# Two two-layer blocks on one core: when the next layer's weights are split, in which order the first rows arrive, and how one value product is formed

## The chip, the cores and the metric

The kernel runs on one core of a Trainium2 chip. The metric is the device time of one execution in microseconds (us). The engines are named as in the profile: PE is TensorE (matrix products), PEld its weight load, DVE is VectorE, ACT is ScalarE, POOL is GpSimd, SP is the engine whose queue issues every DMA of this kernel. A time in the text without a unit is in us from the start of the span.

## The reference

An activation `x` of 512 tokens by 2048 features passes through four layers, two of one block type and then two of another. Each layer is

```
h    = rms_norm(x, g_pre)                 # second block: times (1 + scale), plus shift
proj = h @ w_in                           # 2048 -> 5952 or 5648 columns
o    = several attentions and gates on proj
y    = o @ w_out                          # 2048 -> 2048
x    = x + rms_norm(y, g_post)            # second block: times gate
```

In the second block one of the mixers is a gated linear attention with four heads. Written as one causal product over all 512 tokens, a head's output of 128 tokens is the sum, over the earlier chunks of 128 tokens, of a 128 x 128 score block times the value block of that chunk: 1, 2, 3 and 4 products for the four chunks, 10 for a head. All of it is float32 and has to come out as float32.

## The kernel before

**The products.** A float32 operand is split into a high part that is rounded to the matmul's type (`ACT` copies it) and a low part, the rest (`DVE` subtracts). A product of two split operands is three matmuls: high by high, high by low, low by high (`mm3`, L667). The split of an activation or weight of 128 x 512 costs one ACT and one DVE instruction (`split`, L654). Weights stream from HBM in slots of up to 512 KB into three staging buffers (`st`), are split into `big` tiles or, for a few slots of the first group of a layer, into small tiles `ws`; `Stream.pump` (L563) splits every slot that its window admits and issues the DMAs of the next ones. A staging buffer takes its next DMA only when both parts of its split are done, and SP's queue is in order, so what stands behind that DMA waits too.

**The order of the work.** The program is a single list for each engine, written while the kernel is built. A planner (`Model`, `Side`) keeps an estimated clock for each engine. Large projections are written straight out; between their matmuls `tick` runs steps of side jobs (generators) whose due time has passed. Urgent jobs are run first, about 1 us of planned time after they are due. Only the order comes from the planner; on the chip each engine runs its list in order and waits for semaphores.

**Between layers.** The last quarter of `w_out` (`o3`) and the first group of the next layer (`a_k`, 256 columns, 16 tiles of 128 features, four slots of weights) are computed by blocks of 128 tokens, block 0 to 3 (`by_tokens`, L719). For a block, `o3` takes 48 matmuls of 512 columns (eight slots of weights) and `a_k` 48 of 256. When a block of `o3` is out, an urgent `chain` (L904) is added: the norm after the layer (`y` from `y`, `m`, `x`), four sums of squares on ACT for the next layer's norm, its scaling (`x` from `y`, `m`, `row`), and for each 512 features four transposes on PE, the high part on ACT (`Xh`) and the low part on DVE (`Xl`). Block b of `a_k` needs chain b. In block 3 of `o3`, after each of its eight slots, `pump` splits the weights of `a_k` (L746 to L748).

**The opening.** `first_x` (L845) issues the DMAs of the four blocks of `x` and of the gain rows and the first weights, in the order x0, gain rows, x1, two weight slots, x2, a third slot; then writes the whole norm and transposition of block 0, the sums of squares of block 1, the split of the first weight slot, and the DMA of x3. `pre` (L816) is that norm: four sums of squares on ACT, scaling on DVE (`h`), transposes, split. The jobs of blocks 1 to 3 are independent of each other and run from the ticks of `a_k`.

**The value product of the linear attention.** `out` (L1948) splits the values `V` of a head into a high and a low tile and forms the 10 products with `mm3`, so 30 matmuls of 128 columns, into one PSUM bank; one ACT copy of 128 x 512 takes it out (`og`). There are eight such heads in the kernel, four in each layer of the second block.

Of the kernel before, what the change touches and what calls it, by code (L numbers as in the profile page):

```python
# [9 lines left out]
F32R = mybir.dt.float32r  # L10
I32 = mybir.dt.int32
AF = mybir.ActivationFunctionType
ALU = mybir.AluOpType
# [146 lines left out]
NPAD = 1  # L160
MODT = 1000.0
SHARE = 30.0
BUSY = 0.75
TICK = 3.41333
LOG = None
# [199 lines left out]
class Side:  # L365
# [46 lines left out]
    def step(self, jobs, force):  # L412

        m = self.model
        now = m.clock["PE"]
        nxt = None
        for j in jobs:
            t = j.at()
            spare = (SPARE1 if j.stage else SPARE0) if not force else 0 if j.stage else 4
            if t is None or not self.space(j, 0 if j.urgent else spare):  # L420
                continue
            if t + (SEM if force else SLACK) <= now and (force or j.urgent or self.fits(CAP) and m.free("at", 4, now + 0.1)):
                self.run_one(j)
                return None
            nxt = t if nxt is None else min(t, nxt)
        return -1.0 if nxt is None else nxt

    def start(self, rate):

# [66 lines left out]
class Stream:  # L496
# [86 lines left out]
    def load(self, n):  # L583
        while self.dp < n:
            self.dma(self.items[self.dp])
            self.dp += 1
# [12 lines left out]
class Kern:  # L599
# [119 lines left out]
    def by_tokens(self, parts, need=None, sides=False):  # L719

        st = self.stream
        its = [[] for p in parts]
        self.side.keep = 0
        ahead = NW + 1 if sides else NW
        st.hold = True
        for b in range(4):
            if need and b == 3:
                st.hold = False
            if need:
                self.side.finish([need[b]])  # L730
                self.model.clock["PE"] = max(self.model.clock["PE"], need[b].ready)
            c = slice(b * 128, b * 128 + 128)
            for p, ((spec, evac), mine) in enumerate(zip(parts, its)):
                n, slots = spec
                last = slots[-1][0] + slots[-1][1] - 1
                ps = self.pj()
                for i, (k0, kc, off) in enumerate(slots):
                    if b == 0:
                        mine.append(st.take(sides and 0 < i < 4))
                        st.pump(ahead)  # L740
                    for k2 in range(kc):
                        k = k0 + k2
                        self.mm3(ps[:, :n], [t[:, c] for t in self.Xk(k)], mine[i]["hl"][k2], k == 0, k == last)
                        if k < last:
                            self.side.tick()
                    if b == 3:  # L746
                        st.used(mine[i])
                        st.pump(ahead)  # L748
                evac(b, ps)
                self.side.tick()  # L750
        self.side.keep = SPAREM
# [61 lines left out]
        return f  # L813


    def pre(self, s, xn, tmp, nxt):  # L816

        nc = self.nc
        ss = self.m(4)
        for j in range(4):  # L820
            nc.scalar.activation(self.junk, xn[j], AF.Square, accum_out=ss[:, j:j + 1])
        tot = self.m(1)
        nc.vector.tensor_reduce(tot, ss, axis=AX.X, op=ALU.add)
        r = self.rstd(tot, 1, 1.0 / D)
        yield
        sh = nxt.get("shift")
        for j in range(4):
            nc.vector.scalar_tensor_tensor(tmp[j], xn[j], r, nxt["rows"][j], op0=ALU.mult, op1=ALU.mult)
        for j in range(4):
            yield tmp[j]  # L830
            ps = self.at()
            for i in range(4):
                self.tr(ps[:, i * 128:i * 128 + 128], tmp[j][:, i * 128:i * 128 + 128])
            cs = slice(s * 128, s * 128 + 128)
            xh, xl = self.Xh[:, j * 4:j * 4 + 4, cs], self.Xl[:, j * 4:j * 4 + 4, cs]
            if sh is None:
                self.split(xh, xl, ps.rearrange("p (k t) -> p k t", k=4))
            else:
                cols = [(i, ps[:, i * 128:i * 128 + 128], sh[:, j * 4 + i:j * 4 + i + 1]) for i in range(4)]
                for i, p, c in cols:  # L840
                    nc.scalar.activation(xh[:, i], p, AF.Identity, bias=c)
                for i, p, c in cols:
                    nc.vector.scalar_tensor_tensor(xl[:, i], p, c, xh[:, i].bitcast(F32), op0=ALU.add, op1=ALU.subtract)

    def first_x(self, nxt):  # L845
        nc, I = self.nc, self.I
        xs = [[] for s in range(4)]

        def load(s):
            for j in range(4):  # L850
                t = self.s(name="x")
                nc.sync.dma_start(t, I["x"][s * 128:s * 128 + 128, j * 512:j * 512 + 512])
                xs[s].append(t)

        load(0)
        nxt = nxt()
        load(1)
        self.stream.load(2)
        load(2)
        self.stream.load(3)  # L860
        tmp = [[self.s(name="h") for j in range(4)] for s in range(4)]
        jobs = [self.side.add(self.pre(s, xs[s], tmp[s], nxt), urgent=True) for s in range(4)]

        while not jobs[0].done:
            self.side.run_one(jobs[0])
        self.side.run_one(jobs[1])
        self.stream.pump(1)
        load(3)
        return jobs

    def out_proj(self, PL, l, gains, resid, sink, nxt):

# [677 lines left out]
    def block2(self, l, nxt, chains):  # L1550
        nc, I, side = self.nc, self.I, self.side
# [5 lines left out]
        cs = lambda i: slice(i * 128, i * 128 + 128)  # L1557
# [26 lines left out]
        half = [slice(0, 64), slice(64, 128)]  # L1584
# [258 lines left out]
        cv = [None] * 4  # L1843
# [42 lines left out]
        def gla(dch, after):  # L1886
# [61 lines left out]
            def out(hh):  # L1948
                h = 2 * dch + hh
# [11 lines left out]
                yield  # L1961
                ad = self.hl(name="ad")
                self.split(ad[0], ad[1], A[hh])
                V = self.hl((128, 4, 128), name="V")
                self.split(V[0], V[1], cv[h])
                yield
                blk = lambda t_, i: (t_[0][:, cs(i)], t_[1][:, cs(i)])
                terms = [
                    [(0, blk(ad, 0))],
                    [(1, blk(ad, 1)), (0, blk(fa, 0))],  # L1970
                    [(2, blk(ad, 2)), (0, blk(fa, 1)), (1, blk(fb, 0))],
                    [(3, blk(ad, 3)), (0, blk(fa, 2)), (1, blk(fb, 1)), (2, blk(fa, 3))],
                ]
                ps = self.at()
                for c in range(4):
                    for j, (s, a) in enumerate(terms[c]):
                        self.mm3(ps[:, cs(c)], a, (V[0][:, s], V[1][:, s]), j == 0, j == len(terms[c]) - 1)
                t = self.s(name="og")
                nc.scalar.activation(t, ps, AF.Copy)
                yield  # L1980
                ss = self.m(4)
                junk = self.junk
# [211 lines left out]
```

## Time and profile before

| | |
|---|---|
| three runs | 3278.84, 3280.24, 3283.54 us (median 3280.24) |
| profiled execution | 3280.62 us |
| its span, first to last instruction | 3278.8 us, 45385 instructions |
| PE busy | 3234.3 us (99%), 16666 matmuls |
| DVE, ACT, POOL busy | 2014.3 (61%), 1433.3 (44%), 68.9 us (2%) |
| mean granted clock of PE | 0.996 |
| DMA | 459.00 MB, mean 140 GB/s |
| chain that ended last | PE 95%, DVE 2%, DMA 1%, ACT 1%, issue 1% |

PE is busy in nearly the whole span, so the span is PE's work plus the time in which it waits or runs at a lower clock. The waits of PE say where that is. "Matmul start to matmul start" is the measure of a matmul here, since matmuls overlap and the duration of one in the trace holds its pipeline. All instructions carry the line of one recording helper (L314), so a group is told by its tiles.

### The profile page before, as it was taken

To read this page: it belongs to the slowest core of one execution; us is meant where nothing else is said; L and a number is where in the kernel's file an instruction comes from. 1 tells how busy PE (TensorE), PEld (TensorE's weight loads), DVE (VectorE), ACT (ScalarE), POOL (GpSimd) and SP (SyncE) were. 2 spreads that over 40 slices of the span, in tenths; PEclk is the share of its full clock that TensorE was granted. 3 is DMA by queue.
4 is the path that set the end of the run, shared out by engine and by line. 5 is a ranking of instruction groups with operands and counts; after the bars stand their busy time and mean duration, and the time that the engine had idled before them with its cause. 6 is when DMAs were issued, how large, how long until landed. Compare 5 with 4: busy or idle time off the path is not lost.

```text
span 3278.8 us, 45385 instructions
## 1 busy us (share of the span) xinstructions
PE 3234.3 (99%) x16666; PEld 2761.2 (84%) x16666; DVE 2014.3 (61%) x4788; ACT 1433.3 (44%) x3389; POOL 68.9 (2%) x92
## 2 busy tenths in 40 slices
PE   7999999999999999999999999999999999999998
PEld 7898888888889888888888888888888888888887
DVE  5575655765647676577556577876536466667433
ACT  4444434443434543444345345544435354544331
POOL 0000000000000000000000000000000000000000
PEclk9999999999999999999999999999999999999999
DMA  4443353455544334435563443222445223223344
GB/s 164 145 149 135 135 186 113 145 204 200 178 160 144 128 138 166 146 131 182 194 228 131 142 145 132 97 78 97 164 127 166 92 78 92 77 90 97 127 140 158
DMA packets 186578, 459.00 MB, mean 140 GB/s; under 512 B 22162, under 2 KB 29172, under 8 KB 186356
## 3 DMA queue, kind: packets, MB, share of 16 engines
q1 hardware_dynamic: 186356, 456.11, 41.1%
q8 instruction: 131, 2.15, 0.3%
q14 instruction: 91, 0.75, 0.1%
HBM read 422.44 MB, written 33.59 MB: 139 GB/s over the span
## 4 chain that ended last, share of the span: by engine, by line
PE 95%; DVE 2%; DMA 1%; ACT 1%; issue 1%; SPq 0%; POOL 0%; DVEq 0%; POOLq 0%; ACTq 0%
PE pj L314 79%; PE at L314 16%; DVE Xl L314 1%; ACT junk L314 1%; DVE y L314 1%; DMA st<-in_w 1%; DVE big L314 0%; DMA x<-in_x 0%; DVE x L314 0%; DVE h L314 0%; DMA x<-xs 0%; DVE kT L314 0%; ACT big L314 0%; ACT Xh L314 0%; DVE m L314 0%
## 5 line engine op out<-in xcount | busy, mean ns | idle before, releaser
L314 PE MATMUL pj<-big,Xh 128*128 128x512 f32 (+3 forms) x5152 | 1489.7, 373 | 7.7 <-ACT big L314 4.1
L314 PEld LDWEIGHTS pj<-big,Xh 128*128 128x128 f32 x5152 | 929.5, 189 | 163.8 <-ACT big L314 4.5
L314 PE MATMUL pj<-big,Xl 128*128 128x512 f32 (+3 forms) x2576 | 956.1, 371 | 0.2 <-DVE Xl L314 0.2
L314 PE MATMUL pj<-Xh,big 128*128 128x512 f32 x2816 | 917.6, 394 | 0.0
L314 DVE TENSOR_TENSOR big<-st,big 128x512 fp32r<-128x512 f32 x956 | 600.6, 676 | 352.1 <-ACT big L314 350.5
L314 PEld LDWEIGHTS pj<-Xh,big 128*128 128x128 f32 x2816 | 529.1, 188 | 106.6
L314 ACT ACTIVATE big<-st 128x512 fp32r<-128x512 f32 x956 | 529.4, 616 | 175.3 <-DMA st<-in_w 104.9
L314 PEld LDWEIGHTS pj<-big,Xl 128*128 128x128 f32 x2576 | 485.6, 188 | 83.1 <-DVE Xl L314 0.4
L314 PE MATMUL pj<-Xl,big 128*128 128x512 f32 x1408 | 549.2, 390 | 0.0
L314 PEld LDWEIGHTS pj<-Xl,big 128*128 128x128 f32 x1408 | 265.1, 188 | 48.7
L314 DVE CUSTOM_DVE_ANT_0 wm<-wm,c 128x512 f32<-128x512 f32 x384 | 257.0, 685 | 52.7 <-DMA wm<-in_wm 52.4
L314 ACT ACTIVATE big<-at 128x512 fp32r<-128x512 f32 (+2 forms) x192 | 99.6, 552 | 174.0 <-PE at L314 173.6
L314 DVE TENSOR_TENSOR big<-at,big 128x512 fp32r<-128x512 f32 (+2 forms) x192 | 115.7, 629 | 92.9 <-ACT big L314 92.4
L314 ACT ACTIVATE o<-at 128x256 f32<-128x256 f32 (+2 forms) x104 | 48.0, 465 | 247.4 <-PE at L314 247.0
L314 DVE TENSOR_TENSOR y<-pj,row 128x512 f32<-128x512 f32 x64 | 44.2, 690 | 177.9 <-PE pj L314 177.8
L314 ACT ACTIVATE junk<-pj 128x512 f32<-128x512 f32 x64 | 38.4, 600 | 250.8 <-DVE y L314 250.8
L314 POOL TENSOR_TENSOR m<-m,mhalf 128x1 f32<-128x1 f32 (+2 forms) x88 | 68.7, 784 | 3203.6 <-DVE m L314 3186.3
L314 PE MATMUL pj<-ws,Xh 128*128 128x256 f32 (+1 forms) x480 | 112.2, 327 | 0.0
L314 PE MATMUL at<-kT,qT 128*128 128x128 f32 (+2 forms) x448 | 90.4, 330 | 0.0
L314 PEld LDWEIGHTS at<-big,va 128*128 128x128 f32 x640 | 85.1, 191 | 4.9
L314 DVE TENSOR_REDUCE m<-at 128x1 f32<-128x512 f32 x96 | 65.9, 687 | 37.7 <-PE at L314 37.2
L314 PEld LDWEIGHTS pj<-ws,Xh 128*128 128x128 f32 x480 | 81.3, 191 | 7.5
(227 smaller groups left out, 3062.9 us busy)
## 6 DMA issues: line engine op xcount, KB each, us to landing
st<-in_w SPq DMA_DIRECT2D x472, 512.0 KB, 3.7
wm<-in_wm SPq DMA_DIRECT2D x384, 256.0 KB, 4.2
og<-th SPq DMA_DIRECT2D x64, 256.0 KB, 4.3
st<-og SPq DMA_DIRECT2D x32, 512.0 KB, 3.8
xs<-y SPq DMA_DIRECT2D x48, 256.0 KB, 2.9
x<-in_x SPq DMA_DIRECT2D x32, 256.0 KB, 6.0
x<-xs SPq DMA_DIRECT2D x32, 256.0 KB, 5.4
st<-in_w SPq DMA_DIRECT2D x16, 320.0 KB, 2.8
```

Of the source, the lines that this page charges most:

```text
L314: return f(*a, **k)
```

## The change

Three edits.

1. In `by_tokens`, in block 3 of a group that does not wait for chains (that is `o3`), `pump` after a slot is left out when an urgent job that has begun is due within `HOLD` = 1.5 us of the planner's PE clock.
2. The opening: the first two weight slots are issued ahead of x1, the third behind it; x2 and x3 behind the split of the first weight slot. One of the four sums of squares of a block (the fourth) goes to DVE (`na=3`). The split of the first weight slot stands between the second and the third 512 features of block 0, and the norm of block s+1 begins inside block s; the jobs depend on each other in order.
3. In `out`, the values' high and low parts lie side by side in one tile, so that the high part of a score block is multiplied by both in one matmul of 256 columns, and the low part by the high values in one of 128 columns: 20 matmuls for a head in place of 30. High-by-high and high-by-low come out in neighbouring columns of PSUM, in two banks of two chunks each; ACT copies the one and DVE adds the other.

```diff
+    def soon(self, t):
+        now = self.model.clock["PE"]
+        return any(j.urgent and j.stage and j.at() is not None and j.at() <= now + t for j in self.jobs)
...
                     if b == 3:
                         st.used(mine[i])
-                        st.pump(ahead)
+                        if need or not self.side.soon(HOLD):
+                            st.pump(ahead)
...
-    def pre(self, s, xn, tmp, nxt):
+    def pre(self, s, xn, tmp, nxt, na=4):
...
         for j in range(4):
-            nc.scalar.activation(self.junk, xn[j], AF.Square, accum_out=ss[:, j:j + 1])
+            if j % 2 == 0 or j < 2 * na - 4:
+                nc.scalar.activation(self.junk, xn[j], AF.Square, accum_out=ss[:, j:j + 1])
+            else:
+                nc.vector.tensor_tensor_reduce(out=tmp[j], in0=xn[j], in1=xn[j], scale=1.0, scalar=0.0,
+                                               op0=ALU.mult, op1=ALU.add, accum_out=ss[:, j:j + 1])
...
         load(0)
         nxt = nxt()
+        self.stream.load(2)
         load(1)
-        self.stream.load(2)
-        load(2)
         self.stream.load(3)
         tmp = [[self.s(name="h") for j in range(4)] for s in range(4)]
-        jobs = [self.side.add(self.pre(s, xs[s], tmp[s], nxt), urgent=True) for s in range(4)]
+        gens = [self.pre(s, xs[s], tmp[s], nxt, 3) for s in range(4)]
+
+        def block(s):
+            yield next(gens[s])
+            if 0 < s < 3:
+                next(gens[s + 1])
+            yield from gens[s]
+            if s == 0:
+                next(gens[1])
+
+        jobs = []
+        for s in range(4):
+            jobs.append(self.side.add(block(s), jobs[-1:], urgent=True))
+        next(gens[0])
+        for i in range(3):
+            self.side.run_one(jobs[0])
+        self.stream.pump(1)
+        load(2)
+        load(3)
         while not jobs[0].done:
             self.side.run_one(jobs[0])
-        self.side.run_one(jobs[1])
-        self.stream.pump(1)
-        load(3)
         return jobs
...
-                V = self.hl((128, 4, 128), name="V")
-                self.split(V[0], V[1], cv[h])
+                V = [self.s((128, 2, 2, 128), F32R, "V") for i in range(2)]
+                for i in range(2):
+                    self.split(V[i][:, :, 0], V[i][:, :, 1], cv[h][:, 2 * i:2 * i + 2])
...
-                ps = self.at()
-                for c in range(4):
-                    for j, (s, a) in enumerate(terms[c]):
-                        self.mm3(ps[:, cs(c)], a, (V[0][:, s], V[1][:, s]), j == 0, j == len(terms[c]) - 1)
                 t = self.s(name="og")
-                nc.scalar.activation(t, ps, AF.Copy)
+                for half in range(2):
+                    ps = self.at()
+                    p4 = ps.rearrange("p (c i e) -> p c i e", c=2, i=2)
+                    for c in (2 * half, 2 * half + 1):
+                        for j, (s, a) in enumerate(terms[c]):
+                            v = V[s // 2][:, s % 2]
+                            end = j == len(terms[c]) - 1
+                            if j > 0:
+                                nc.tensor.matmul(p4[:, c % 2, 0], lhsT=a[1], rhs=v[:, 0], start=False, stop=False)
+                            nc.tensor.matmul(p4[:, c % 2], lhsT=a[0], rhs=v, start=j == 0, stop=end and j > 0)
+                            if j == 0:
+                                nc.tensor.matmul(p4[:, c % 2, 0], lhsT=a[1], rhs=v[:, 0], start=False, stop=end)
+                    tc = t[:, half * 256:half * 256 + 256].rearrange("p (c e) -> p c e", c=2)
+                    nc.scalar.activation(tc, p4[:, :, 0], AF.Copy)
+                    nc.vector.tensor_tensor(tc, tc, p4[:, :, 1], op=ALU.add)
```

## Rows read from the trace of the kernel before

**Rows 1.** Waits of PE, whole span: us in total, times, longest.
```profile
PE at L314 <- DVE h L314: 11.8, 2, 10.4
PE at L314 <- DVE x L314: 11.4, 5, 3.3
PE pj L314 <- ACT big L314: 4.1, 1, 4.1
```

**Rows 2.** Busy time by stretch, opening: engines in order, PEclk, DMA share, GB/s.
```profile
10.45:31.00 20.55, 13.79 (x81) 12.43 (x81) 13.23 (x26) 16.06 (x39) 1.48 (x3) 1.00 0.88 319
...
34.30:42.70 8.40, 6.90 (x32) 6.50 (x33) 8.19 (x13) 4.04 (x7) 0.00 (x0) 0.50 0.01 2
```

**Rows 3.** Timeline of ACT in the opening: start, us, what, idle before.
```profile
12.45 0.60 ACT L314 ACTIVATE Xh<-at 128x512 fp32r<-128x512 f32 x1 [0.25 <-PE at L314]
...
14.65 0.62 ACT L314 ACTIVATE junk<-x 128x512 f32<-128x512 f32 x1
...
17.53 2.17 ACT L314 ACTIVATE big<-st 128x512 fp32r<-128x512 f32 x4
...
29.44 0.63 ACT L314 ACTIVATE junk<-x 128x512 f32<-128x512 f32 x1
...
53.47 0.38 ACT L314 ACTIVATE kr<-pj 128x256 f32<-128x256 f32 x1 [5.38 <-PE pj L314]
```

**Rows 4.** Timeline of DVE in the opening.
```profile
9.64 2.74 DVE L314 SCALAR_TENSOR_TENSOR h<-x,m,row 128x512 f32<-128x512 f32 x4 [0.67 <-POOL m L314]
...
24.99 2.73 DVE L314 SCALAR_TENSOR_TENSOR h<-x,m,row 128x512 f32<-128x512 f32 x4
```

**Rows 5.** Timeline of SP's queue in the opening, third and fourth weight slot.
```profile
13.15 6.68 SPq L314 DMA_DIRECT2D st<-in_w  x2
```

**Rows 6.** DMA issues of the page: weights, count, KB each, us to landing.
```profile
st<-in_w SPq DMA_DIRECT2D x472, 512.0 KB, 3.7
```

**Rows 7.** The chain that ended last, first boundary: four transpositions.
```profile
890.37 0.44 PE at L314 x4
```

**Rows 8.** Timeline of DVE at the second boundary between layers.
```profile
1730.87 1.29 DVE L314 TENSOR_TENSOR ws<-st,ws 128x512 fp32r<-128x512 f32 x2 [1.54 <-ACT ws L314]
1732.08 2.73 DVE L314 SCALAR_TENSOR_TENSOR y<-y,m,x 128x512 f32<-128x512 f32 x4
...
1739.25 0.16 DVE L314 TENSOR_REDUCE m<-m 128x1 f32<-128x4 f32 x1 [2.68 <-ACT junk L314]
...
1749.22 2.73 DVE L314 SCALAR_TENSOR_TENSOR x<-y,m,row 128x512 f32<-128x512 f32 x4
```

**Rows 9.** Timeline of PE at the second boundary, `o3` into `a_k`, to `a_v`.
```profile
1730.97 0.62 PE L314 MATMUL pj<-big,Xh 128*128 128x512 f32 x2
...
1731.65 0.40 PE L314 MATMUL pj<-big,Xh 128*128 128x256 f32 x2
...
1732.01 0.40 PE L314 MATMUL pj<-big,Xh 128*128 128x256 f32 x2
...
1750.02 3.33 PE L314 MATMUL at<-ident,x 128*128 128x128 f32 x16 [3.32 <-DVE x L314]
...
1763.61 0.41 PE L314 MATMUL pj<-big,Xh 128*128 128x272 f32 x2
```

**Rows 10.** Timeline of PE at the third boundary: first of `a_k`, first of `a_v`.
```profile
2503.12 0.40 PE L314 MATMUL pj<-big,Xh 128*128 128x256 f32 x2
...
2537.29 0.41 PE L314 MATMUL pj<-big,Xh 128*128 128x272 f32 x2
```

**Rows 11.** Timeline of PE, first row of the last head's value product, first behind it.
```profile
3054.67 0.79 PE L314 MATMUL at<-V,ad 128*128 128x128 f32 x6
...
3057.97 0.44 PE L314 MATMUL pj<-Xh,big 128*128 128x512 f32 x1
```

**Rows 12.** Busy time by stretch, around the first heads: columns as in rows 2.
```profile
2120.00:2330.00 210.00, 210.00 (x1094) 178.26 (x1094) 139.97 (x314) 95.62 (x214) 7.39 (x8) 1.00 0.27 93
```

**Rows 13.** Groups of instructions on DVE: busy us, mean ns, idle before.
```profile
L314 DVE TENSOR_TENSOR pad<-E,pad 128x256 fp32r<-128x256 f32 x26 | 10.9, 419 | 3.0 <-ACT pad L314 2.9
```

More of the change, by code (lines that the diff above doesn't have):

```diff
@@ L162 @@
 SHARE = 30.0
+HOLD = 1.5
 BUSY = 0.75
```

## The prediction

> **What bounds the kernel now.** The profile's page comes first: PE is busy 99% of the span and makes up 95% of the chain that ended last, so time can go in two ways only, by less work on PE or by shorter waits of PE (with the low clock that follows them). The waits of PE for the whole span come next [rows 1]. The reader is to see how short the list is: 10.4 us before the first transposition, which is the arrival of x and the first norm; then 1.4 more on `h` and 4.1 on `big`, in the opening too; and 11.4 on `x` in five waits, all at the three boundaries between layers. Everywhere else PE waits for nothing, so an engine that gets work there costs nothing while it keeps up. Third, the stretches of the opening by granted clock [rows 2]: from 34.3 PE runs 8.4 us at 0.50, the lower of its two levels (1.2 GHz), right behind its waits, so a wait there costs more than its own length.
>
> **Edit 3, the value product.** The last head's 30 matmuls of 128 columns take 3057.97 - 3054.67 = 3.30 us, 0.110 from start to start [rows 11]. Matmuls of 256 columns start 0.36 / 3 = 0.120 apart, of 512 columns 0.68 / 3 = 0.227 apart [rows 9]. From 512 to 256 columns the time halves, from 256 to 128 it hardly falls: a narrow matmul pays for being one. A term now costs 3 x 0.110 = 0.33 us and will cost 0.120 + 0.110 = 0.23; ten terms, eight heads: 80 x 0.10 = 8.0 us off PE. The unknown is how a wide and a narrow one mix. At best the narrow one costs in proportion to its columns, 0.06, and 80 x 0.15 = 12 us go; at worst the three parts cost what they cost now, and nothing goes. I take 8.0, the two rows as they stand.
>
> [...]
>
> Beside it, each head pays on ACT two half copies in and two out at some 0.38 (the copy of 256 columns, [rows 3]) for two whole ones at 0.54 (four in 2.17, [rows 3]), and on DVE two half splits and two half additions at 0.42 [rows 13] for one whole split at 0.65 (two in 1.29, [rows 8]): 0.4 on ACT and 1.0 on DVE, 8 us on DVE over all heads. DVE is busy 140 of 210 us around the heads while PE is busy all 210 [rows 12], so I cost it at nothing; without that cover it is the 8 us, and edit 3 is worth nothing. The two banks in one step can make PE wait for an evacuation, at most the 0.8 of a half copy and a half addition a head.
>
> **Edit 2, the opening.** `a_k` ends 48 x 0.12 = 5.8 us after its third block, which is copied out at 53.47 [rows 3]: at 59.2. Now the new order, engine by engine.
> - Block 0: the fourth square on DVE (0.69, as a pass of `h`, [rows 4]) runs beside three on ACT, where four take 17.53 - 14.65 = 2.9, 0.72 each [rows 3]; x arrives meanwhile, so I take half of one as gained: `h` starts at 9.3 in place of 9.64 [rows 4].
> - First weights: the second high part starts at 12.45 and takes 0.60 [rows 3], 0.3 earlier now; the split of slot 1 follows on ACT (2.17 / 4 = 0.54 each, two of them): 12.8 to 13.9, its DVE half ends at 14.8. PE starts on `a_k` at about 13.9. In the trace that split begins only at 17.53, behind four squares of block 1 [rows 3].
> - Squares of block 1: the rest of block 0 takes ACT to 15.1, three squares to 17.4, then slots 2 and 3 to 19.6. The DMA of slot 4 waits for the staging buffer of slot 1: 14.8 now, 19.8 before, the end of the pair [rows 5]; with 3.7 to land [rows 6] it is there at 18.5, its split is done at 21.9 on DVE. Cover: PE has slots 1 to 3 until then, with waits of 1 to 3 us that the start at 13.9 pays for.
> - Block 1: `h` 21.9 to 24.6 (24.99 to 27.7 before, [rows 4]). ACT now does three squares of block 2 ahead of the high parts of block 1; before, it did the squares of blocks 2 and 3 first, and the eighth begins at 29.44 [rows 3]. DVE does the fourth square of block 2 and the two small steps (1.1 us), and the first low part is there at 26.4.
> - From there PE is the longer: three blocks of 5.76 and two sets of 16 transpositions at 0.11 [rows 7]. DVE needs 2.73 + 1.1 + 2.75 = 6.6 us a block, PE 7.5. So 26.4 + 17.3 + 3.5 = 47.2, and 1 us for what doesn't mesh: 48.2.
>
> 59.2 - 48.2 = 11.0 us. What is moved on SP's queue: x1 stands behind 1 MB of weights, 3.3 us at the 319 GB/s of the stretch [rows 2]; counted from 2 us with x0, the gain rows and these ahead of it, 4 MB land by about 14.5, just ahead of its squares at 15.1; x2 and x3 wait for slot 4's place at 14.8 and land by about 20 and 22, ahead of theirs. If x1 came 2 us later, so would all from block 1 on. The bounds: should PE stay on the lower level through block 1, as it did until 42.7 [rows 2], the 5.8 us double, and 5 to 6 are left; with no wait at all behind 13.9 DVE sets the end and 13 go.
>
> **Edit 1, the boundaries.** From the start of `a_k` to that of `a_v` it is 1763.61 - 1731.65 = 32.0 us at the second boundary [rows 9] and 2537.29 - 2503.12 = 34.2 at the third [rows 10]; four blocks and the transpositions of two are 4 x 5.76 + 3.5 = 26.5. So 5.5 and 7.7 us are lost, 13.2 in all; the first boundary loses nothing there. The place is the last scaling, of block 3, at 1749.22 [rows 8]: PE waits 3.32 for it and then runs 16 transpositions in 3.33 in place of 1.76 [rows 9]. Upstream DVE has idled 1.54 and 2.68 [rows 8]: the norm of block 2 (1732.08) stands behind the split of the fourth slot, which waits for its DMA; so its squares come after block 3's, and block 3's steps behind them. Held back, `pump` runs in the gaps that the planner sees (VectorE backed up by over 1.5 us, or four squares under way), for the first slots; the rest goes to the start of `a_k`, where `take` forces it. The norm of block 2 then starts 2.5 to 5 us earlier, its squares run within `o3`, DVE's gaps close, and block 3's scaling moves to about 1745. PE needs it at 1731.65 + 17.3 + 1.7 = 1750.6: the wait is gone. What is late next is the split of the last slots; DVE needs 1.29 for one, PE uses one in 1.44, so they hold the pace once begun. I leave 1.8 us at each of these boundaries for a slot or first tile that is late, and take 13.2 - 3.7 = 9.5. Ends: 13.2, and a loss, which is a rival below.
>
> **Sum.** 3280.6 (the profiled execution; 3278.8 of span and 1.8 around it, 0.4 above the median of the runs) - 8.0 - 11.0 - 9.5 = **3252 us**.
>
> **Rivals.**
> - *The hold changes little.* VectorE is backed up at the second and third boundary, so a step is due later than 1.5 us, `pump` still runs slot after slot, and the norm stays behind the splits. For: the norm has begun, and yet the splits stand ahead of it now [rows 8]. Against: one slot less ahead is enough to take out the wait for the DMA. Gain 2 there: 3260. Chance 0.15.
> - *The opening stays bound by DVE and the low clock.* For: DVE is busy 8.19 of the 8.40 us from 34.3 [rows 2], and gets four squares more. Gain 4 to 5: 3258. Chance 0.12.
> - *Columns set the time of a narrow matmul*, and edit 3 takes nothing off PE: 3280.6 - 11.0 - 9.5 = 3260. The 0.110 [rows 11] beside the 0.120 [rows 9] speaks against it. Chance 0.06. [...]
> - *Starved start, the slower side.* The chain is always due, no slot is split in `o3`, and at all three boundaries `a_k` begins with none: PE waits 1.8 for the first (1.1 on ACT, 0.65 on DVE), about 1 for the fourth, whose DMA is issued only then, and the chains stand behind eight splits (5.2 us of DVE), so block 2 waits about 5; with 3 at the lower level some 11 a boundary, 33 in all: 3280.6 - 8 - 11 + 33 = 3295. It decides for slower from 19 / 3 = 6.3 a boundary. Against: four squares take 3 us, a gap longer than 1.5. Chance 0.03.
>
> **How the numbers follow.** The forecast, 3246 to 3258, has 0.58; the single rivals 0.15, 0.12, 0.06, 0.03; two of the first three together, 3264 to 3270, 0.06. Range for 8 in 10: 3244 to 3266. A measurement of this kernel tells 0.2%, 6.6 us, from no change. Of the 28.5 us, 22 would have to be lost for it not to show: faster 0.93, within it 0.04, slower 0.03.
>
> **What would show it.** Right: first matmul of `a_k` near 14 and `a_k`'s end near 48; ACT's squares in groups of three; no wait of PE on `x` at block 3 of `a_k`, and 27 to 29 us from `a_k` to `a_v` at the second and third boundary; 2.3 us for a head's 20 matmuls. Wrong: waits of PE on `big` or `ws` at the start of `a_k`; a new wait of PE on an evacuation at the heads; or PEclk of 0.5 beyond 30 us.

## Result, and the profile after

| | before | after |
|---|---|---|
| median of four runs | 3281.4 us | 3244.3 us (3242.5 to 3246.1) |
| ratio to before | | 0.9886 (95%: 0.9873 to 0.9898) |
| span of the profiled execution | 3278.8 | 3241.8 |
| PE busy, matmuls | 3234.3, 16666 | 3215.1, 16586 |
| mean granted clock | 0.996 | 0.999 |

The change gains 37 us where 28.5 were forecast: 3244 lies below the forecast of 3246 to 3258. The waits of PE after, whole span (us in total, times, longest), are the answer to [rows 1]:

```profile
PE at L315 <- DMA row<-in_g: 10.1, 1, 10.1
PE at L315 <- DVE x L315: 2.7, 3, 1.0
PE at L315 <- issue: 2.1, 1, 2.1
PE pj L315 <- DVE big L315: 1.0, 3, 0.4
PE pj L315 <- ACT big L315: 1.0, 1, 1.0
...
PE at L315 <- DVE h L315: 0.4, 1, 0.4
```

The 11.4 us on `x` have become 2.7, the 4.1 on `big` 1.0. Where the 37 us lie is read from the same instructions in both traces. Each trace is one execution, and the four runs of one kernel lie up to 4.7 us apart, so single entries of 1 to 2 us are not certain:

| instruction (start, us) | before | after | gained by then | in the stretch | forecast for it |
|---|---|---|---|---|---|
| third copy of `kr` (opening) | 53.47 | 41.55 | 11.9 | 11.9 | 11.0 |
| first of `a_k`, second boundary | 1731.65 | 1715.59 | 16.1 | 4.1 | 0 |
| first of `a_v`, second boundary | 1763.61 | 1742.32 | 21.3 | 5.2 | 9.5 with the other one |
| first of `a_k`, third boundary | 2503.12 | 2476.82 | 26.3 | 5.0 | 4.0, four heads |
| first of `a_v`, third boundary | 2537.29 | 2504.79 | 32.5 | 6.2 | (above) |
| end of the span | 3278.8 | 3241.8 | 37.0 | 4.5 | 4.0, four heads |

**Opening.** First the two stretches of [rows 2] (columns as there), then timelines of ACT (two parts), DVE and SP, the answers to [rows 3 to 5]:

```profile
10.13:31.00 20.87, 18.32 (x121) 16.53 (x122) 19.63 (x38) 17.23 (x38) 1.50 (x2) 1.00 0.88 322
34.30:42.70 8.40, 8.40 (x74) 8.40 (x73) 4.51 (x8) 3.57 (x8) 0.00 (x0) 1.00 0.01 2
```

```profile
12.76 1.15 ACT L315 ACTIVATE big<-st 128x512 fp32r<-128x512 f32 x2
...
41.55 0.38 ACT L315 ACTIVATE kr<-pj 128x256 f32<-128x256 f32 x1 [3.72 <-PE pj L315]
...
21.28 2.73 DVE L315 SCALAR_TENSOR_TENSOR h<-x,m,row 128x512 f32<-128x512 f32 x4
...
10.91 4.24 SPq L315 DMA_DIRECT2D st<-in_w  x2
```

The first weights are split at 12.76 in place of 17.53, the fourth slot's DMA is out at 10.91 + 4.24 = 15.15 in place of 19.83, block 1's `h` starts at 21.28 in place of 24.99, and in the second stretch PE is busy throughout at a clock of 1.00, where it ran at 0.50.

**A boundary.** Timeline of DVE at the second boundary, the answer to [rows 8]:

```profile
1709.53 1.30 DVE L315 TENSOR_TENSOR big<-st,big 128x512 fp32r<-128x512 f32 x2 [0.17 <-ACT big L315]
1710.76 1.28 DVE L315 TENSOR_TENSOR ws<-st,ws 128x512 fp32r<-128x512 f32 x2
1711.96 2.73 DVE L315 SCALAR_TENSOR_TENSOR y<-y,m,x 128x512 f32<-128x512 f32 x4
1714.61 2.48 DVE L315 TENSOR_TENSOR ws<-st,ws 128x512 fp32r<-128x512 f32 x4
```

Two slots (`big` x2 and `ws` x2) stand ahead of the norm of block 2 and two behind it; before, all four stood ahead. Timeline of PE at the third boundary, `a_k` to `a_v`:

```profile
2476.82 0.40 PE L315 MATMUL pj<-big,Xh 128*128 128x256 f32 x2
...
2494.13 1.32 PE L315 MATMUL at<-ident,x 128*128 128x128 f32 x8 [1.03 <-DVE x L315]
...
2504.79 0.41 PE L315 MATMUL pj<-big,Xh 128*128 128x272 f32 x2
```

The wait at block 3 is 1.03 in place of 3.32 (at the second boundary there is none), and the transpositions behind it run at the full clock, 8 in 1.32. From `a_k` to `a_v` it is 28.0 us here and 26.7 at the second boundary.

**A head.** Timeline of PE, first row of the first head's value product and first row behind it, the answer to [rows 11]:

```profile
2129.79 0.57 PE L315 MATMUL at<-V,ad 128*128 128x256 f32 x4
...
2132.09 0.45 PE L315 MATMUL at<-pad,pad 128*128 128x128 f32 x3
```

20 matmuls in 2.30 us; all eight heads are 3.30 before and 2.30 after.

**What was not forecast.** The stretch ahead of the second `a_k` holds the transpositions of block 0 of `o3`. Timelines of PE, their first rows at the three boundaries, before and then after:

```profile
852.33 1.95 PE L314 MATMUL at<-ident,x 128*128 128x128 f32 x12 [2.26 <-DVE x L314]
...
1701.12 1.75 PE L314 MATMUL at<-ident,x 128*128 128x128 f32 x8 [2.42 <-issue]
...
2474.55 1.95 PE L314 MATMUL at<-ident,x 128*128 128x128 f32 x12 [1.25 <-DVE x L314]
```

```profile
839.59 1.95 PE L315 MATMUL at<-ident,x 128*128 128x128 f32 x12 [0.72 <-DVE x L315]
...
1686.79 0.63 PE L315 MATMUL at<-ident,x 128*128 128x128 f32 x4 [2.10 <-issue]
...
2448.84 2.04 PE L315 MATMUL at<-ident,x 128*128 128x128 f32 x12 [0.97 <-DVE x L315]
```

The first wait is 1.5 us shorter. The second is hardly shorter, but before it was followed by a stretch at the lower clock (8 transpositions took 1.75) and after it was not; together 2.1. Nothing in the change is written at this place. (`issue` means that the view found no releaser. In both traces the norm of block 0 had waited for the DMA of its residual rows shortly before, see `e7_resid_early`.)

### The profile page after: what moved, and what is told of

It is laid out like the page before. It is cut to its first block, busy times and chain, and to the rows that moved or that the text cites. A ratio compares the mean times of both kernels' runs of the same rounds, so it can differ in the third digit from the quotient of the medians.

```text
span 3241.8 us, 45249 instructions
## 1 busy us (share of the span) xinstructions
PE 3215.1 (99%) x16586; PEld 2744.3 (85%) x16586; DVE 2021.2 (62%) x4820; ACT 1432.7 (44%) x3397; POOL 68.1 (2%) x92
## 4 chain that ended last, share of the span: by engine, by line
PE 97%; DVE 1%; DMA 1%; ACT 0%; issue 0%; SPq 0%; POOL 0%; DVEq 0%; POOLq 0%; ACTq 0%
PE pj L315 81%; PE at L315 16%; DMA x<-in_x 0%; DVE y L315 0%; DVE big L315 0%; DVE Xl L315 0%; DMA row<-in_g 0%; ACT junk L315 0%; DMA st<-in_w 0%; DMA x<-xs 0%; DVE h L315 0%; SPq L315 0%; DVE kT L315 0%; ACT kT L315 0%; ACT big L315 0%
## 5 line engine op out<-in xcount | busy, mean ns | idle before, releaser
L315 ACT ACTIVATE big<-at 128x512 fp32r<-128x512 f32 (+1 forms) x192 | 99.4, 552 | 183.8 <-PE at L315 183.2
L315 DVE TENSOR_TENSOR big<-at,big 128x512 fp32r<-128x512 f32 (+1 forms) x192 | 115.7, 629 | 97.9 <-ACT big L315 97.5
```

The costliest lines, as they stand in the source:

```text
L315: return f(*a, **k)
```

## Experiments

Each was timed in five rounds beside the kernel before (3281.2 to 3282.6 in these). Times are medians; "3.0 later" is the profiled instruction against the same one of the kernel after.

### One edit at a time

`e1_hold_only`, `e2_opening_only` and `e3_value_only` are the kernel before with one edit of the diff each; `e4_without_hold` is the kernel after without edit 1.

> The kernel before with edit 1 alone. The gain of the whole change, 37.0 us of span, was 8.5 more than forecast; 3.8 of the excess lies in o3, at the transpositions of block 0, ahead of anything that the hold can move at that boundary. Theory A (the planner's clock: whatever changes the program earlier moves where a step falls later, so waits at block 0 of o3 are set by chance): the 2.26 us wait at the first boundary stays, the third block's delays at the second and third boundary go (11.4 us between a_k and a_v), time 3268 to 3271. Theory B (the hold is worth all that was gained at the boundaries, 15 to 16 us): 3265 to 3267, and the 2.26 us wait is below 1. Rival of the prediction (the hold changes little): 3279.

> The kernel before with edit 2 alone. By the sum of parts a_k of the first layer ends 11.9 us earlier, at 47.3. Theory A: the later order is shifted too, so a wait at block 0 of some o3 changes, 1.5 us at the first boundary (2.26 to 0.72) and up to 2 at the second: 3265.5 to 3269.5. Theory B: nothing behind the opening changes, the 2.26 stays: 3269 to 3270.

> The kernel before with edit 3 alone. Eight heads at 1.00 us each (30 matmuls in 3.30 us, 20 in 2.30): 8.0, with up to 0.3 for what else moves: 3273. The first two layers have no such head, so the waits of PE up to the second boundary are those of before to the digit (2.26 at the first). If columns set the time of a narrow matmul: 3281.

> The kernel after with edit 1 taken out (pump after every slot). Theory A: block 0 of o3 at the first boundary still waits 0.7 and not 2.26, and between a_k and a_v the second and third boundary take 32 and 34 us again: 3254 to 3258. Theory B: all 15 to 16 us at the boundaries come back: 3259 to 3261. Rival (hold changes little): 3246.

| | us | ratio to before | wait at block 0, boundary 1, 2, 3 | wait at block 3, boundary 2, 3 |
|---|---|---|---|---|
| before | 3281.4 | | 2.26, 2.42, 1.25 | 3.32, 3.32 |
| e1, hold | 3270.5 | 0.9965 (0.9952 to 0.9977) | 2.07, 3.03, 2.07 | none, none |
| e2, opening | 3266.9 | 0.9956 (0.9943 to 0.9968) | 0.28, 2.53, 1.27 | 3.32, 3.32 |
| e3, value | 3273.3 | 0.9976 (0.9966 to 0.9985) | 2.07, 2.13, 2.74 | 3.33, 3.45 |
| e4, all but the hold | 3260.5 | 0.9933 (0.9920 to 0.9947) | 0.74, 2.29, 2.29 | 3.32, 3.32 |
| after | 3244.3 | 0.9886 (0.9873 to 0.9898) | 0.72, 2.10, 0.97 | none, 1.03 |

The hold takes away the waits at block 3 (1.03 stays at the third boundary of the kernel after); the "hold changes little" rival is out. The first boundary's wait at block 0 changes with the opening (0.28), not with the hold (2.07), as theory A has it. By time theory A has e1 and e2, and e3 came out at its 3273, while e4 fell into theory B's range, since block 0 got worse too: 2.29 for 0.97 at the third boundary, and at the second a wait of about the same length (2.29 for 2.10), but with the low clock behind it. The lists of e3 are those of the kernel before up to the second boundary, so its waits there were forecast "to the digit"; they are 2.07 and 2.13 in place of 2.26 and 2.42. Differences of 0.3 at one place therefore say nothing. Alone the edits gain 10.7, 14.4 and 7.9 us, 33.0 in all; together 37.

At two boundaries the waits at block 0 go with where PE's list has the transpositions. Counted in projection matmuls ahead of the first of them, at the first boundary: 3150 in e6 and the two kernels built on it (waits 2.1 to 3.3), 3153 in before, e1 and e3 (2.1 to 2.3), 3156 in the three with early residual rows (0.3 to 0.4), 3159 in after and eight others (0.3 to 1.0). At the third, without the early rows: 9486 (2.6 to 2.7), 9489 (2.1 to 2.3), 9492 (1.3 to 2.2), 9495 (0.6 to 1.1). Three matmuls of 512 columns are 0.68 us. The planner puts them by its clock, and its clock at a boundary depends on all that was written earlier. At the second boundary the place does not tell: eleven kernels have the same one, 6417, and wait 1.9 to 3.0, and three more have it with the early rows and wait 0.96 or 0.97.

### The parts of the opening

`e6_square_act`, all squares on ACT:

```diff
-        gens = [self.pre(s, xs[s], tmp[s], nxt, 3) for s in range(4)]
+        gens = [self.pre(s, xs[s], tmp[s], nxt, 4) for s in range(4)]
```

> The kernel after, with all four sums of squares of a block on ACT in the opening, as before. The prediction counted half a pass for it at block 0 (0.35 us) and otherwise cover, PE being longer than ACT from block 1 on: 0.3 to 0.8 more, a_k ends at 47.6 to 48.1 in place of 47.3. Rival (the square on DVE carries the opening, since ACT would be busy 6.0 of 7.5 us a block and the high parts come late): 2 to 5 more.

3259.2 (0.9927, 0.9914 to 0.9939), 15 more, and no theory had that. The opening itself is 0.2 us earlier, and the third copy of `kr` lies anywhere from 41.3 to 43.0 in the kernels with the same opening as the kernel after: the square on DVE is worth nothing there that can be seen. Nearly all of the loss is at the boundaries, where no line differs: 3.0 at the first, 4.4 at the second, 6.7 at the third. Block 0 stands 9 matmuls earlier in the list of the first boundary (wait 2.64, low clock behind it), at the second it waits 3.50, and at the third three slots came ahead of the norm of block 2 in place of one and the wait at block 3 is back:

```profile
2504.92 3.48 PE L315 MATMUL at<-ident,x 128*128 128x128 f32 x16 [3.42 <-DVE x L315]
```

`e16_late_split` (on the count and order described below, which set the boundaries):

```diff
-        self.stream.pump(1)
-        load(2)
-        load(3)
         while not jobs[0].done:
             self.side.run_one(jobs[0])
+        self.stream.pump(1)
+        load(2)
+        load(3)
```

> Two slots and the order forced, and in the opening the split of the first weight slot (with x2 and x3 behind it) moved to the end of block 0, in place of between its second and third 512 features. By the prediction's steps the split is 1.2 us of ACT and the staging place of slot 4 comes free when it is done: a_k starts 2 later, its end 1.5 to 3 later than 47.3 (the fourth slot's DMA goes out later by as much). Rival (the opening's gain is the order of the DMAs and of the squares, not this): its end moves by under 0.7.

`a_k` starts 3.9 later (forecast 2) and the third copy of `kr` is at 44.53, 3.0 later, and 1.5 to 3.2 against the other kernels with the opening of the kernel after; the rival is out. The whole is 3250.1; in the profiled executions the boundaries lost another 5.3, so this total does not price the early split. Timelines of PE and SP:

```profile
17.37 0.58 PE L315 MATMUL pj<-big,Xh 128*128 128x256 f32 x1 [3.32 <-ACT big L315]
...
10.61 8.40 SPq L315 DMA_DIRECT2D st<-in_w  x2
```

The fourth slot's DMA goes out at 19.0 in place of 15.15: the prediction's chain of staging place, DMA and split.

### Wide and narrow matmuls, and a start without splits

`e8_wide_low`, the low part of a score block times both halves (and likewise in the matmul for `j == 0`):

```diff
-                                nc.tensor.matmul(p4[:, c % 2, 0], lhsT=a[1], rhs=v[:, 0], start=False, stop=False)
+                                nc.tensor.matmul(p4[:, c % 2], lhsT=a[1], rhs=v, start=False, stop=False)
```

> The kernel after, with the low part of a score block multiplied by the high and the low values (256 columns, not 128), so that low by low is added too. Theory N (a narrow matmul pays for being one, 0.110 beside 0.120): 80 x 0.010 = 0.8 more, a head takes 2.40, 3245. Rival (columns set the time, 0.056 for 128): 80 x 0.053 = 4.3 more, a head takes 2.83, 3248.6.

A head takes 2.39; first head and first row behind it:

```profile
2131.60 0.64 PE L315 MATMUL at<-V,ad 128*128 128x256 f32 x4
...
2133.99 0.45 PE L315 MATMUL at<-pad,pad 128*128 128x128 f32 x3
```

Ten matmuls of 128 columns made 256 wide cost 0.09 us, 0.009 each, and the whole 3244.8. Twice the columns for nearly nothing: the narrow one pays for being narrow. The Trainium skill, page "TensorE: Matmul & The Clock Gate", section "Back-to-back issue gap", gives columns / 2.4 GHz plus 2.5 ns as the gap of a single matmul, and says itself that this counts too little at few columns: for a stream of weight loads and matmuls it has about 81 ns at 128 columns. By the formula each of the ten would cost 0.053 us more, an estimate; this case has 0.009, and 0.110 at 128 columns is above both of the section's figures (0.056 and 0.081). The measurement decides.

`e5_hold_all`, no split of the next weights in block 3 of `o3`:

```diff
-                        if need or not self.side.soon(HOLD):
+                        if need:
```

> The kernel after, with no split of the next weights in block 3 of o3 at all (as if the hold were endless). Theory S (starved start, the prediction's slower side): a_k begins without a split slot, PE waits about 1.8 for the first and 1 for the fourth, and block 2 of a_k waits about 5 for its norm behind eight splits: 6 to 11 a boundary, 3262 to 3277. Rival (the splits of four slots take DVE 5.2 us and a_k is longer than that, so only the first slot's wait shows, 1.8 a boundary): 3247 to 3252.

3260.0 (0.9933, 0.9920 to 0.9945), 15.7 more, between the two theories. PE waits 2.08 for the first slot at each boundary, and 1.82 more for its low part at the second; in the profiled execution the three boundaries cost 4.5, 8.5 and 4.7 more than in the kernel after. Endless holding is as bad as none (e4, 3260.5), but the prediction's slower side had 3295 for it.

### The residual rows of block 0

`e7_resid_early`:

```diff
         xl = [self.side.add(load_x(0), urgent=True)]
+        self.side.finish(xl[:1])
```

> The kernel after, with the residual rows of block 0 issued ahead of the first weights of o3 in place of behind four of them. Theory D (the 2.1, 1.0 and 0.7 us that PE still waits at block 0 of o3 come from that DMA: y of block 0 stands 2.1 us on x<-xs at the third boundary): the waits of the second and third boundary go, 3 us, 3241; the first is not set by it and stays. Theory A (the planner's clock alone sets them): the waits are still 1 to 3 us each, 3243 to 3247.

3240.7 (0.9872, 0.9859 to 0.9886). Timelines of SP and of DVE's norm of block 0 at the second boundary, after and then e7:

```profile
1669.71 5.98 SPq L315 DMA_DIRECT2D st<-in_w  x4
1675.74 10.09 SPq L315 DMA_DIRECT2D x<-xs  x16
...
1680.09 0.75 DVE L315 SCALAR_TENSOR_TENSOR y<-y,m,x 128x512 f32<-128x512 f32 x1 [1.00 <-DMA x<-xs]
```

```profile
1657.34 5.66 SPq L315 DMA_DIRECT2D x<-xs  x8
1668.63 6.47 SPq L315 DMA_DIRECT2D st<-in_w  x4
...
1678.74 2.74 DVE L315 SCALAR_TENSOR_TENSOR y<-y,m,x 128x512 f32<-128x512 f32 x4 [0.73 <-POOL m L315]
```

In the kernel after, the rows stand behind four weight DMAs, and the norm waits for them, 1.00 us ahead of its first step and 0.9 more between its steps. Ahead of those DMAs they no longer hold it up, and PE's wait falls from 2.10 to 0.96. At the third boundary the planner put the transpositions 9 matmuls earlier (9486 for 9495) and the wait is 1.54 in place of 0.97; at that place kernels without the early rows wait 2.6 to 2.7. The wait at its block 3 fell to 0.22. So theory D holds for the second boundary, and at the third the list's order took back what the rows gave; the 3241 came out, but not as the "3 us" of two waits that go.

### What makes the wait at block 3 of `a_k`

In e6 the hold failed at the third boundary, so the condition by planned times was replaced by a count: two slots may be split ahead of the norm of block 2, the others behind it (`e9_rule`; with e6's squares `e10_rule_square`; with e7's rows `e11_rule_resid`; with three slots `e12_rule_three`).

```diff
-                        if need or not self.side.soon(HOLD):
+                        if need or i < 2 or first():
...
-        self.by_tokens([(PL["o3"], last)], sides=True)
+        self.by_tokens([(PL["o3"], last)], sides=True, first=lambda: nxt is None or chains[2].stage > 1)
```

> The kernel after, with a count in place of the planner's clock: in block 3 of o3 two slots may be split ahead of the norm of block 2 (y), the others behind it. Theory C (how many slots stand ahead of that norm is what matters: with three or four PE waits 3.3 to 3.5 at block 3 of a_k, with none to two at most 1): no wait over 1.1 there, the waits at block 0 of o3 are still of 0.3 to 3, 3242 to 3248. Rival (the hold worked by its planned times, and two slots at the first and third boundary, where the kernel after has none and one, cost): a wait of over 2 there, 3248 to 3254.

> The count of two slots, with the four sums of squares of the opening on ACT, beside 3259.2 with these squares and the hold. There three slots stood ahead of the norm at the third boundary, and PE waited 3.4. Theory C: that wait and the low clock behind it go, 4 to 5.5 less, 3253 to 3256; the waits at block 0 of o3 (2.6, 3.5 and 1.6 there) are not touched by the count and stay of that order. Rival (the square on DVE is what the boundaries need): 3257 to 3260.

> The count of two slots with the early residual rows, beside 3240.7 with the hold and the early rows. Both have no wait over 1.6 at any boundary, so the two are equal within 2 us: 3239 to 3243. If the count is the worse rule: 3244 to 3248.

> The count with three slots ahead of the norm of block 2 in place of two. Theory C with its edge between two and three: PE waits 3.3 to 3.5 at block 3 of a_k at the second and third boundary, with 0.7 to 2 of low clock behind each: 8 to 11 more than with two, 3251 to 3257. Rival (only the fourth slot, whose DMA comes late, makes the wait): as with two, 3242 to 3248.

e9 3243.9, e11 3241.3, as theory C had it; e12 3258.1 with waits of 3.45 at both boundaries, 14 more than e9 (forecast 8 to 11, the rest being waits at block 0 of 2.8 and 2.6). But e10 took 3257.3, the rival's range: with two slots ahead PE waited even longer at the third boundary. So the count is not the cause. Timelines of DVE, and then of PE (first matmul of `a_k`, transpositions of block 3), there, e10:

```profile
2483.90 2.73 DVE L315 SCALAR_TENSOR_TENSOR y<-y,m,x 128x512 f32<-128x512 f32 x4
2486.55 2.49 DVE L315 TENSOR_TENSOR ws<-st,ws 128x512 fp32r<-128x512 f32 x4
2488.96 0.68 DVE L315 TENSOR_TENSOR y<-pj,row 128x512 f32<-128x512 f32 x1
2493.54 0.16 DVE L315 TENSOR_REDUCE m<-m 128x1 f32<-128x4 f32 x1 [3.90 <-ACT junk L315]
...
2505.06 2.74 DVE L315 SCALAR_TENSOR_TENSOR x<-y,m,row 128x512 f32<-128x512 f32 x4 [0.73 <-POOL m L315]
...
2486.08 0.40 PE L315 MATMUL pj<-big,Xh 128*128 128x256 f32 x2
...
2505.86 2.82 PE L315 MATMUL at<-ident,x 128*128 128x128 f32 x12 [4.16 <-DVE x L315]
```

The evacuation of block 3 (`y<-pj`) stands ahead of the four squares of block 2, and both reduces come behind it, with DVE idle for 3.90. Theory O: that order decides. `e13_order_square` is e10 with the squares of block 2 written ahead of that evacuation:

```diff
+                if b == 3 and norm:
+                    norm()
                 evac(b, ps)
...
+        def norm():
+            self.side.finish(xl[2:3])
+            while chains[2].stage < 3:
+                self.side.run_one(chains[2])
...
```

`e14_order_no_hold` is the kernel after with this order, but no hold and no count; `e15_order_resid` is order, count and early rows.

> The count of two slots with the squares of the opening on ACT took 3257.3 and still waited 4.2 at block 3 of a_k at the third boundary, with two slots ahead of the norm of block 2, so the number of slots is not the cause (theory C fell). Theory O: what decides is whether the sums of squares of block 2 stand in the lists ahead of the evacuation of block 3 of o3 or behind it. Here they are forced ahead of it, all else as there. Theory O: no wait over 1.1 at block 3 of a_k, 4 to 6 less, 3251 to 3253; the waits at block 0 stay. Rival (DVE is simply late by the waits of block 0): a wait of 3 or more stays, 3256 to 3259.

> The kernel after without the hold, all four slots split ahead of the norm of block 2 as before, but the sums of squares of block 2 forced ahead of the evacuation of block 3; 3260.5 without that. Theory O alone: no wait over 1.1 at block 3, 9 to 12 less, 3248 to 3252. Rival (four slots ahead make the norm itself too late): the wait of block 2's own chain shows instead, or block 3's stays over 2, and 3254 to 3261.

> Two slots, the order of squares forced, and the early residual rows. The lists at the boundaries are those that the count gave with the early rows (3241.3), so 3239 to 3243; a version whose order does not hang on the planner's clock.

The same of e13 at the third boundary:

```profile
2482.56 2.73 DVE L315 SCALAR_TENSOR_TENSOR y<-y,m,x 128x512 f32<-128x512 f32 x4
2485.21 2.49 DVE L315 TENSOR_TENSOR ws<-st,ws 128x512 fp32r<-128x512 f32 x4
2489.18 0.16 DVE L315 TENSOR_REDUCE m<-m 128x1 f32<-128x4 f32 x1 [1.48 <-ACT junk L315]
...
2489.44 0.68 DVE L315 TENSOR_TENSOR y<-pj,row 128x512 f32<-128x512 f32 x1
...
2501.73 2.74 DVE L315 SCALAR_TENSOR_TENSOR x<-y,m,row 128x512 f32<-128x512 f32 x4 [0.73 <-POOL m L315]
...
2484.73 0.40 PE L315 MATMUL pj<-big,Xh 128*128 128x256 f32 x2
...
2502.53 1.32 PE L315 MATMUL at<-ident,x 128*128 128x128 f32 x8 [1.03 <-DVE x L315]
```

The norm of block 2 (`y<-y,m,x`) starts 2.2 us ahead of `a_k` in both. In e13 the reduce of block 2 is there at 2489.18, ahead of the evacuation, and 4.16 has become 1.03: 3250.6 in place of 3257.3 (forecast 3251 to 3253), although its waits at block 0 (3.27, 3.26, 1.89) are no shorter on the whole than e10's (2.12, 3.19, 2.21). Of the 3.13 us, 2.0 are DVE's: the last scaling (`x<-y,m,row`) starts 17.0 us behind the start of `a_k` in place of 19.0. The other 1.15 are PE's: its wait begins 16.77 us behind that start in place of 15.62, since with the forced order the transpositions of block 3 also stand later in PE's list, behind 120 matmuls of `a_k` in place of 108.

e14 takes 3248.8 where without order and hold it was 3260.5, but it still waits 1.60 and 2.21 at block 3, more than forecast: four slots ahead of the norm do cost something. There the last scaling starts 17.1 and 18.5 us behind the start of `a_k`, where it was 17.7 and 17.8 in e4, so with four slots ahead most of the shorter wait is PE's later place (120 for 105). All kernels together, second and third boundary; "behind" means that the squares of block 2 come behind block 3's evacuation, and "place" is the number of matmuls of `a_k` ahead of block 3's transpositions in PE's list:

| kernel | slots ahead of the norm | squares of block 2 | place | wait at block 3 |
|---|---|---|---|---|
| before, e2, e4 | 4, 4 | behind, behind | 105, 105 | 3.32, 3.32 |
| e3 | 4, 3 | behind, behind | 105, 108 | 3.33, 3.45 |
| e12 | 3, 3 | behind, behind | 105, 108 | 3.45, 3.45 |
| e6 | 1, 3 | ahead, behind | 120, 105 | none, 3.42 |
| e10 | 2, 2 | ahead, behind | 120, 108 | none, 4.16 |
| e14 | 4, 4 | ahead, ahead | 120, 120 | 1.60, 2.21 |
| e16 | 2, 2 | ahead, ahead | 120, 120 | 0.95, 0.96 |
| after, e8, e9, e13 | 2, 1 or 2 | ahead, ahead | 120, 120 | none, 1.0 |
| e7 | 2, 1 | ahead, ahead | 120, 120 | none, 0.22 |
| e1, e11, e15 | 2, 2 | ahead, ahead | 120, 120 | none, none |
| e5 | 0, 0 | ahead, ahead | 111, 120 | none, 0.41 |

Twelve times "behind" (the first row is three kernels), twelve waits of 3.3 to 4.2; no other over 2.3. But wherever the squares are behind, PE's place is 105 or 108, and no run moves the one without the other. What e13 shows is that forcing the order of the steps takes the wait away; how much of it is the order on DVE and how much PE's place is known only from the sums above.

**The better version.** e15 takes 3240.7 (0.9876, 0.9861 to 0.9890) and e7 as much. Their ratios' intervals overlap with that of the kernel after, but every run of either (up to 3241.9) lies below its four (from 3242.5): some 3.6 us, likely but not beyond doubt. e15's boundary order hangs on stages and a count, not on planned times.

## Why the prediction was off, and what of it held

**Edit 3** came out to the digit: 1.00 us a head, 8.0 in all, and 7.9 alone. The pair of 256 and 128 columns costs 0.230, the two rows added. DVE's extra work shows in no wait of PE.

**Edit 2** was worked out step by step and held: first matmul of `a_k` 13.46 (13.9), `h` of block 1 21.28 (21.9), end of `a_k` 41.55 + 5.76 = 47.3 (48.2), full clock. 11.9 for 11.0; the 1 us for what doesn't mesh was not needed. The half pass of the fourth square was nothing that can be seen (e6), and the early split carries 1.5 to 3 (e16).

**The boundaries are the step that failed.** The sum gave them one term, edit 1's "13.2 - 3.7 = 9.5"; measured they brought some 16 us (11.4 + 4.5). The term was mis-sized, and it left out waits.

Mis-sized: between `a_k` and `a_v` 11.4 us went, since only 1.8 of the 3.7 left for lateness was used.

Left out: "Everywhere else PE waits for nothing" passes over rows of the same list of waits before, among them these:

```profile
PE at L314 <- issue: 2.4, 1, 2.4
...
PE pj L314 <- DVE big L314: 1.1, 1, 1.1
```

The 2.4 is at block 0 of `o3` at the second boundary, and 2.26 and 1.25 of the 11.4 us on `x` [rows 1] are at block 0 at the first and the third. Only the remaining 7.9 on `x` lie between `a_k` and `a_v`, the stretch that the sum priced. The waits at block 0, with the low clock behind them, brought 1.5 and 2.1 up to the second `a_k` and 0.2 at the third, and the wait for a split in `a_v` of the second boundary (1.05, now 0.30) 0.7: 4.5 us that the sum put at nothing, without a reason. With the 1.9 between `a_k` and `a_v`, 0.9 in the opening, and 1.2 that was not traced further (half of it in layer 1) this is the 8.5 us.

**The mechanism of edit 1 held in the main.** The prediction's sentence "so its squares come after block 3's, and block 3's steps behind them" names the order that e13 forces, and with it the wait falls from 4.16 to 1.03. The wait for the fourth slot's DMA, from which the prediction derived that order, is not needed for it: e12 and e10 have the long wait with three and two slots ahead. It also read PE's need wrongly. "1731.65 + 17.3 + 1.7 = 1750.6" puts block 3's transpositions behind three whole blocks of `a_k`, 144 matmuls; PE's list has them behind 105 before and behind 120 after. At the second boundary PE asked 15.0 us behind the start of `a_k` before and 16.1 after, not 19. The last scaling after starts 15.3 us behind that start at the second boundary, in time, and 16.5 at the third, where PE waits 1.03.

**The left-out part is largely luck.** Nothing in the edits aims at block 0. The 1.5 at the first boundary came with the opening's edit (wait 0.28 in e2, 0.74 in e4), as a later place in the list. Nearly all of the 2.1 at the second boundary is the low clock, which followed a wait of 2.42 in the profiled execution of the kernel before and not the 2.10 in that of the kernel after. And e6 has the same three edits but for a square that costs its opening nothing, and gains 23. At the first and third boundary the waits at block 0 go with the place in PE's list (3150, 3153, 3159), which the planner's clock sets anew after an edit ahead of it; at the second they hang on the DMA of the residual rows (e7). The forecast treated the planner's order outside the edits as fixed; each boundary held 1 to 4 us that were open either way, and the hold itself, a condition on planned times, failed at one boundary in e6.

**The rivals.** "The hold changes little" is out where the order of squares comes right; at one boundary of e6 it happened. "Bound by DVE and the low clock" is out (8.40 of 8.40 us at 1.00). "Columns set the time" is out by e8. "Starved start" did not come, and e5, which forces it, takes 3260 in place of 3295.

## What to carry to other kernels

Price every row of the list of waits, also those that the edit doesn't touch, and say for each whether it could move. Where a planner's clock sets the order, an edit far ahead can cost or bring more than itself (15 us here from one that was worth 0.2): compare the lists of the engines at the places that matter, and fix the order there by stages and counts, not by planned times. And where a late norm makes PE wait, look first at which block's reduce stands ahead of which block's evacuation on DVE and at where PE's own list asks for the result, and then at how much work stands between.

## What the runs showed of the hardware

Equal waits do not always bring the lower clock. At block 0 of the first boundary PE waited 2.07 in both e1 and e3, which have the same place in the list there. The granted clock of the 6 us from 1 us ahead of these transpositions was 0.72 in e1 (852 to 858) and 1.00 in e3 (851 to 857).

At block 0 of the second boundary PE waited 2.10 in the kernel after and 2.29 in e4, at the same place in the list. The stretch from 1686 to 1692 (columns as in rows 2), after and then e4:

```profile
1686.00:1692.00 6.00, 5.21 (x31) 4.58 (x32) 6.00 (x17) 4.35 (x16) 0.00 (x0) 1.00 0.87 273
```

```profile
1686.00:1692.00 6.00, 5.01 (x23) 4.55 (x24) 5.24 (x14) 3.74 (x15) 0.10 (x1) 0.72 0.89 277
```

The clock column reads 1.00 in one and 0.72 in the other, and e4 had lost 1.8 us by the start of `a_k`, 0.2 of it the wait. Nor was it the longer wait that brought the lower clock: at this boundary e2 waited 2.53 and stayed at 1.00 (1686 to 1692), and e16 waited 1.82 and shows 0.72 (1689 to 1695). A forecast can give a wait of about 2 us its own length and, as a chance, some 1.6 us more.
